# A decoder layer's first feed-forward product: from seven block products to plain tiles of 128 columns

## The chip, the cores and the metric

The kernel runs on one core of a Trainium2 chip. Its time is the device time of one execution in microseconds (us); the median of several executions is compared. TensorE multiplies (its stationary operand is loaded by separate weight loads), ScalarE and VectorE work element by element and read TensorE's results from PSUM, GpSimd (POOL in the profile) issues the DMAs that add, and SyncE (SP) issues the loads. Each engine has its own queue of instructions, which it works through in order.

## What is computed

One decoder layer on x of 512 positions by 1024 channels: two mixers, a merge, an output projection, a layer norm, and then a feed-forward block with a second layer norm. The change touches the feed-forward block only:

```python
    h = layer_norm(DEEPNORM_ALPHA * h + mix, ln1_g[l], ln1_b[l])
    f = jnp.square(jax.nn.relu(h @ w_ff1[l])) @ w_ff2[l]
    h = layer_norm(DEEPNORM_ALPHA * h + f, ln2_g[l], ln2_b[l])
```

w_ff1 is 1024 x 4096 and w_ff2 is 4096 x 1024, in float32. The kernel multiplies float32 numbers as pairs: each operand is split into a high part (a rounded copy) and a low part (the rest), and a product is three matmuls, high x high, high x low and low x high.

## The kernel before

**Stages.** Input projection, mixers and attention come first, then the output projection with the first layer norm (lines 740 to 852), then the feed-forward block in four quarters of 1024 hidden channels. In each quarter q the first product (FF1) makes the quarter's hidden values from h, and the second (FF2) adds their product with 1024 rows of w_ff2 to `hn`. Quarter 3's FF2 is not done in blocks but in plain steps (`b_step`, line 739), so that the layer norm can start early.

**Seven products.** A product of matrices that are cut into 2 x 2 blocks needs eight block products; both FF1 and FF2 use a scheme with seven, on sums of blocks. The seven are called p = 1 to 7. For FF1 the blocks of h (halves of channels by halves of positions) are copied and combined once, by `h_first` and `h_second`, into the pairs `X[p]`. The weight blocks come in column groups n of 512 columns, eight in all: `ff1_blocks` and `du_chunks` load each group into three tiles: U (two blocks, in the ring of buffers called raw), V (one block) and S (one block, twice). Sums are formed in place by DMAs that add, issued by POOL (`dma_add`): `s13` adds U's blocks to S; after the split for p = 1 S is added into U; after the split for p = 2 U is added into V. So each group has four adding DMAs, and the weights of p = 6, 7, 3 and 5 exist only when these have landed. FF2 does the same with blocks of w_ff2 (`ff2_blocks`), two halves h per quarter.

**Weight stream.** `Stream` holds a list of items in the order of use. `ws.get()` returns the next one's high and low parts and prepares two items ahead: `split` copies the float32 weights on ScalarE (line 150) and subtracts on VectorE (line 151), into one of three buffers `whi`, `wlo`. A tile is loaded when its ring has a free slot: raw, V and S have two each. In the time order of one engine everything queues: a load that waits for its slot holds back SP's later loads.

**FF1's products.** `ff1_product` (line 863) does 24 matmuls of 256 moving columns: two halves j of 128 weight columns, four channel tiles k, three matmuls each (lines 879, 881, 882). The moving operand is a block of h of 256 positions. The results of several p accumulate in one PSUM bank; ScalarE or VectorE takes them out, and `rest`, done one product later, applies relu and square and writes the blocks `Y[c]` of the hidden values that FF2 multiplies (`y_split`). A quarter has 14 such products. `ff2_product` (line 934) does per half h 12 matmuls of 512 columns (lines 947, 949, 950), and VectorE adds each p's two banks to `hn`.

**Order.** Tile's scheduler orders the instructions by their place in the program and its own model of times, so the last FF1 product of a quarter stands a few matmuls behind the first ones of FF2. Plain products with weights as the stationary operand use `dense_a` and `mm3` (lines 132 to 135): eight channel tiles of three matmuls with 512 moving columns:

```python
    def dense_a(ps, piece, mh, ml, c0=0, c1=S):
        hi, lo = piece
        for k in range(8):
            mm3(ps[:, c0:c1], hi[:, k], lo[:, k], mh[:, k, c0:c1], ml[:, k, c0:c1], k == 0, k == 7)
```

## Time and profile before

| | us |
|---|---|
| median of 3 runs (924.97 to 927.46) | 926.69 |
| the profiled execution | 929.51 |
| its span, from first to last instruction | 927.8 |
| TensorE busy | 884.8 |
| VectorE busy | 550.9 |
| ScalarE busy | 408.7 |
| GpSimd busy | 51.3 |

The profile is of one execution. Its span is the time from the first to the last instruction; the rest of the execution's time lies around it. Busy times of matmuls overlap, since TensorE starts one before the last has left it, so the pace of TensorE is read from the starts of its matmuls. A wait is put down to what came last of the things that an instruction waited for.

### The profile page before, as it was taken

The page shows a single profiled execution, that of the slowest core. Times are in us where ns is not written, and L with a number is a line of the kernel's source. Part 1 is how long each engine was busy: PE and PEld are TensorE (multiplying, and loading weights), DVE is VectorE, ACT ScalarE, POOL GpSimd, SP SyncE. Part 2 cuts the span into 40 slices and gives each one's busy share as a digit, 9 for nine tenths or more (in the row PEclk, how much of TensorE's full clock was granted, in tenths as well). Part 3 has the DMA queues.
Part 4 walks back from the last instruction along what each step waited for, and adds up shares of the span by engine and source line. Part 5 has one row for each costly group of instructions (what it writes and reads, how often), then busy time and mean ns, then how long its engine had stood idle before and what let it go on. Part 6 is the DMA issues. An engine that isn't in the chain of part 4 may idle for free. (4 is left out here: it accounts for less than half of the span.)

```text
span 927.8 us, 12312 instructions
## 1 busy us (share of the span) xinstructions
PE 884.8 (95%) x4792; PEld 759.1 (82%) x4792; DVE 550.9 (59%) x1039; ACT 408.7 (44%) x704; POOL 51.3 (6%) x68
## 2 busy tenths in 40 slices
PE   8999999999999999999999998998899989988996
PEld 6888898988887888888788888867887888778984
DVE  2322736442238766767556688784578467745667
ACT  2522313242226556555433146742665267426800
POOL 1000000000000000000000100111021102111000
PEclk9999999999999999999999998999899989998998
DMA  6458501232332111111383923969697969694601
GB/s 199 130 177 239 170 24 47 78 130 91 97 114 64 40 53 46 46 47 46 118 290 130 211 46 92 243 145 272 153 241 153 274 172 236 160 246 110 192 37 68
DMA packets 79865, 125.83 MB, mean 136 GB/s; under 512 B 3328, under 2 KB 55360, under 8 KB 79808
## 3 DMA queue, kind: packets, MB, share of 16 engines
q1 hardware_dynamic: 67232, 88.19, 29.0%
q0 software_dynamic: 8064, 29.36, 16.9%
q10 hardware_dynamic: 4512, 7.50, 2.6%
q8 instruction: 37, 0.61, 0.3%
q14 instruction: 20, 0.16, 0.0%
HBM read 93.59 MB, written 2.10 MB: 103 GB/s over the span
## 5 line engine op out<-in xcount | busy, mean ns | idle before, releaser
L151 DVE TENSOR_TENSOR wlo<-raw,whi 128x1024 fp32r<-128x1024 f32 (+3 forms) x125 | 145.2, 1165 | 184.9 <-ACT whi L150 184.2
L150 ACT ACTIVATE whi<-raw 128x1024 fp32r<-128x1024 f32 (+3 forms) x125 | 126.1, 1012 | 239.5 <-PE ps L134 115.4
L879 PE MATMUL ps<-x,whi 128*128 128x256 f32 x448 | 133.7, 299 | 18.3 <-ACT whi L150 10.1
L882 PE MATMUL ps<-x,wlo 128*128 128x256 f32 x448 | 132.7, 296 | 5.1 <-DVE wlo L151 5.1
L881 PE MATMUL ps<-x,whi 128*128 128x256 f32 x448 | 131.7, 294 | 1.6 <-DVE x L817 1.6
L133 PE MATMUL ps<-xh,whi 128*128 128x512 f32 x320 | 129.6, 405 | 0.0
L134 PE MATMUL ps<-xl,whi 128*128 128x512 f32 x320 | 125.7, 393 | 0.0
L135 PE MATMUL ps<-xh,wlo 128*128 128x512 f32 x320 | 125.7, 393 | 0.0
L879 PEld LDWEIGHTS ps<-x,whi 128*128 128x128 f32 x448 | 90.9, 203 | 22.5 <-ACT whi L150 11.4
L882 PEld LDWEIGHTS ps<-x,wlo 128*128 128x128 f32 x448 | 90.8, 203 | 6.6 <-DVE wlo L151 6.6
L881 PEld LDWEIGHTS ps<-x,whi 128*128 128x128 f32 x448 | 90.9, 203 | 2.2 <-DVE x L817 2.1
L135 PEld LDWEIGHTS ps<-xh,wlo 128*128 128x128 f32 x320 | 60.5, 189 | 13.2
L134 PEld LDWEIGHTS ps<-xl,whi 128*128 128x128 f32 x320 | 60.8, 190 | 9.5
L133 PEld LDWEIGHTS ps<-xh,whi 128*128 128x128 f32 x320 | 60.7, 190 | 9.5
L950 PE MATMUL ps<-wlo,y 128*128 128x512 f32 x144 | 56.9, 395 | 3.3 <-DVE wlo L151 3.3
L947 PE MATMUL ps<-whi,y 128*128 128x512 f32 x144 | 56.7, 394 | 1.4 <-ACT whi L150 1.4
L949 PE MATMUL ps<-whi,y 128*128 128x512 f32 x144 | 56.2, 390 | 0.0
L208 POOL DMA_DIRECT2D S<-raw x28 | 24.3, 890 | 568.9 <-DMA raw<-in_w_ff_dram 539.7
L628 ACT ACTIVATE PP<-PP,nm 128x512 f32<-128x512 f32 (+3 forms) x64 | 35.8, 559 | 35.6 <-DVE nm L622 35.3
L151 DVE TENSOR_TENSOR wlo<-S,whi 128x1024 fp32r<-128x1024 f32 x28 | 34.0, 1222 | 25.0 <-ACT whi L150 24.9
L151 DVE TENSOR_TENSOR wlo<-V,whi 128x1024 fp32r<-128x1024 f32 x28 | 34.2, 1223 | 21.4 <-ACT whi L150 20.5
L150 ACT ACTIVATE whi<-S 128x1024 fp32r<-128x1024 f32 x28 | 29.3, 1055 | 36.6 <-DMA S<-raw 15.8
(223 smaller groups left out, 1745.2 us busy)
## 6 DMA issues: line engine op xcount, KB each, us to landing
raw<-in_w_in_dram SPq DMA_DIRECT2D x17, 1024.0 KB, 5.2
S<-in_w_ff_dram SPq DMA_DIRECT2D x28, 512.0 KB, 6.0
raw<-in_w_ff_dram SPq DMA_DIRECT2D x28, 512.0 KB, 6.2
S<-raw POOLq DMA_DIRECT2D x28, 512.0 KB, 7.5
V<-in_w_ff_dram SPq DMA_DIRECT2D x14, 512.0 KB, 5.0
raw<-S POOLq DMA_DIRECT2D x14, 512.0 KB, 6.3
V<-raw POOLq DMA_DIRECT2D x14, 512.0 KB, 5.3
raw<-in_w_in_dram SPq DMA_DIRECT2D x8, 512.0 KB, 3.6
```

Source lines behind the costliest of these rows:

```text
L133: nc.tensor.matmul(ps, hi, mh, start=start, stop=False)
L134: nc.tensor.matmul(ps, hi, ml, start=False, stop=False)
L135: nc.tensor.matmul(ps, lo, mh, start=False, stop=stop)
L150: nc.scalar.activation(hi, r, AF.Copy)
L151: nc.vector.tensor_sub(lo, r, hi.bitcast(F32))
L628: nc.scalar.activation(t, t, AF.Exp, bias=nm[:, e, i:i + 1], scale=-1.0, accum_out=sm[:, e, i:i + 1])
L879: nc.tensor.matmul(o, hi[:, k, js], xh[:, k], start=opens and j == 0 and k == 0, stop=False, skip_group_check=True)
L881: nc.tensor.matmul(o, hi[:, k, js], xl[:, k], start=False, stop=False, skip_group_check=True)
L882: nc.tensor.matmul(o, lo[:, k, js], xh[:, k], start=False, stop=j == 1 and k == 3, skip_group_check=True)
L947: nc.tensor.matmul(ps, yh, hi[:, kk], start=opens and h == 0 and kk == 0, stop=False, skip_group_check=True)
L949: nc.tensor.matmul(ps, yl, hi[:, kk], start=False, stop=False, skip_group_check=True)
L950: nc.tensor.matmul(ps, yh, lo[:, kk], start=False, stop=h == 1 and kk == 1, skip_group_check=True)
```

## The change

FF1 gets plain tiles. The transposed h is kept whole, as `hTh` and `hTl` (8 channel tiles x 512 positions); `h_transpose` fills them with one copy and one subtraction per bank. A quarter has eight pieces of 128 hidden columns, each one `dense_a`: 24 matmuls of 512 columns (lines 133 to 135), accumulated in one bank. The weights come in loads of 1 MB, each for two pieces (`cols_a`), without sums of blocks: `ff1_blocks`, `ff1_product` and FF1's 32 adding DMAs are gone. From quarter 1 on the first two loads of a quarter go into the S ring, the other two into raw. In quarter 0 three pieces take their high and low parts in the slots of S and V (`early`), are multiplied with positions 0 to 255 first, and with 256 to 511 after the last two transposes. `ff1_evict` takes a piece out of PSUM with Relu and Square on ScalarE and, once per two pieces, writes the block sums `Y[c]` that FF2 wants: the same seven as before. FF2's code does not change. The four vectors of both layer norms are loaded together into `lnc`.

```diff
-    def add(shape, dmas, pieces):
-        c = ws.chunk("raw", shape, dmas)
+    def add(shape, dmas, pieces, ring="raw"):
+        c = ws.chunk(ring, shape, dmas)
...
-    def cols_a(w, c0, ncol, kt=8):
+    def cols_a(w, c0, ncol, kt=8, ring="raw", dsts=(None, None)):
...
-                pieces=[((lambda t, j=j: t[:, :, j * P:(j + 1) * P]), None) for j in range(2)]))
+                pieces=[((lambda t, j=j: t[:, :, j * P:(j + 1) * P]), dsts[j]) for j in range(2)], ring=ring))
...
-                ready=lambda: "lpool" in res)
+                ready=lambda: "rings" in res)
...
-    def ff1_blocks(n):
-        def blk(half, k):
-            c0 = 1024 * (n // 2) + 512 * half + 256 * (n % 2)
-            return w1v[:, 4 * k:4 * k + 4, c0:c0 + 256]
-        return du_chunks([4, 256], blk)
...
-    ffseq, FF2 = [], (1, 2, 6, 5, 7, 3, 4)
+    FF2 = (1, 2, 6, 5, 7, 3, 4)
+    def early():
+        res["early"] = res.get("early", 0) + 1
+        if res["early"] < 3:
+            t = res["lpool"].tile([P, 2, 8, P], F32R, tag="S", bufs=2, name=f"e{res['early']}")
+            return t[:, 0], t[:, 1]
+        hl = [res["lpool"].tile([P, 8, P], F32R, tag="V", bufs=2, name=f"e{res['early']}{i}")
+              for i in range(2)]
+        res["rings"] = True
+        return hl
...
-        du = [2 * q, 2 * q + 1]
...
-        ffseq.append([(2 * q + i, p) for i, p in order])
-        dus = {}
-        for n, p in ffseq[q]:
-            if n not in dus:
-                dus[n] = ff1_blocks(n)
-                du_item(dus[n], p, s13(dus[n]))
-            else:
-                du_item(dus[n], p)
+        for i, c in enumerate((0, 512, 256, 768)):
+            cols_a(w1, 1024 * q + c, 256, ring="S" if q and i < 2 else "raw",
+                   dsts=((early, early if i == 0 else None) if q == 0 and i < 2 else (None, None)))
...
-    def consts(g, b):
-        res["lnc"] = slab("lnc", [P, 2, D])
-        nc.sync.dma_start(res["lnc"][:, 0], bcast(g[0]))
...
+    lnc = slab("lnc", [P, 4, D])
+    for i, t in enumerate((ln1_g, ln1_b, ln2_g, ln2_b)):
+        nc.sync.dma_start(lnc[:, i], bcast(t[0]))
...
+    hTh = slab("hTh", [P, 8, S], F32R)
+    hTl = slab("hTl", [P, 8, S], F32R)
+    def h_transpose(t):
...
-    def x_split(p, src, cs, k4=slice(0, 4)):
-        h, l = X[p][0][:, k4, cs], X[p][1][:, k4, cs]
-        nc.scalar.activation(h, src, AF.Copy)
-        nc.vector.tensor_sub(l, src, h.bitcast(F32))
...
-    def h_first(t):
-        cs = slice(t * P, (t + 1) * P)
-        for p, raw, pt in zip((1, 2), (h11, h21), h_banks(t, "aa")):
-            x_split(p, pt, cs)
-            nc.scalar.activation(raw[:, :, cs], pt, AF.Copy)
...
-    def h_second(t, tags):
-        cs = slice((t - 2) * P, (t - 1) * P)
-        p0, p1 = h_banks(t, tags)
-        nc.scalar.activation(h22[:, :, cs], p1, AF.Copy)
-        t1, t3, t2, t4 = (small_t("T").rearrange("p (k i) -> p k i", k=4) for _ in range(4))
-        nc.vector.tensor_tensor(t1, h11[:, :, cs], p0, op=ALU.subtract)
-        nc.vector.scalar_tensor_tensor(t2, t1, -1.0, h22[:, :, cs], op0=ALU.mult, op1=ALU.subtract)
-        x_split(5, t1, cs)
-        x_split(6, t2, cs)
-        nc.vector.tensor_tensor(t3, h22[:, :, cs], p0, op=ALU.subtract)
-        x_split(3, h22[:, :, cs], cs)
-        nc.vector.scalar_tensor_tensor(t4, t2, -1.0, h21[:, :, cs], op0=ALU.mult, op1=ALU.subtract)
-        x_split(7, t3, cs)
-        x_split(4, t4, cs)
...
+            p3 = pt.rearrange("p (k i) -> p k i", k=4)
+            dh = hTh[:, 4 * q:4 * q + 4, t * P:(t + 1) * P]
+            dl = hTl[:, 4 * q:4 * q + 4, t * P:(t + 1) * P]
+            nc.scalar.activation(dh, p3, AF.Copy)
+            nc.vector.tensor_sub(dl, p3, dh.bitcast(F32))
...
         if t > 1:
-            h_first(t - 2)
...
+            h_transpose(t - 2)
...
+    y4 = lpool.tile([P, 2, D], F32R, tag="y4", bufs=1, name="y4")
+    RR = slab("RR", [P, 2, 2, 2, 512])
...
-    def ff1_product(n, p):
...
-        xh, xl = X[p]
-        for j in range(2):
-            js = slice(j * P, (j + 1) * P)
-            o = ps[:, j * 256:(j + 1) * 256]
-            for k in range(4):
-                nc.tensor.matmul(o, hi[:, k, js], xh[:, k], start=opens and j == 0 and k == 0, stop=False,
-                                 skip_group_check=True)
-                nc.tensor.matmul(o, hi[:, k, js], xl[:, k], start=False, stop=False, skip_group_check=True)
-                nc.tensor.matmul(o, lo[:, k, js], xh[:, k], start=False, stop=j == 1 and k == 3,
-                                 skip_group_check=True)
-        while later:
-            later.pop(0)()
-        if p in (1, 5, 6):
-            g[p] = small_t("b")
-            nc.scalar.activation(g[p], ps, AF.Copy)
...
+    def ff1_evict(q, i, ps, g):
+        if i % 4 == 0:
+            g["R"] = RR[:, i // 4]
+        R = g["R"]
+        r = lpool.tile([P, S], F32, tag="r", bufs=2, name=f"r{q}_{i}")
+        nc.scalar.activation(r, ps, AF.Relu)
+        nc.scalar.activation(R[:, i % 4 // 2, i % 2], r, AF.Square)
+        if i % 2 == 0:
             return
-        if p == 4:
-            t = g["t21"] = small_t("b")
-            nc.scalar.activation(t, ps, AF.Relu, scale=-1.0)
+        rows = slice(2 * (i // 4), 2 * (i // 4) + 2)
+        b11, b12, b21, b22 = (R[:, h, :, c:c + 256] for h in range(2) for c in (0, 256))
+        def y_split(c, t):
+            nc.scalar.activation(Y[c][0][:, rows], t, AF.Copy)
+            nc.vector.tensor_sub(Y[c][1][:, rows], t, Y[c][0][:, rows].bitcast(F32))
+        if i % 4 == 1:
+            y_split(1, b11)
+            if q == 3:
+                y_split(5, b12)
+            else:
+                nc.vector.tensor_sub(b11, b11, b12)
+                y_split(5, b11)
+        elif q == 3:
+            y_split(2, b21)
+            y_split(3, b22)
         else:
-            t = g[{2: 1, 3: 6, 7: 5}[p]]
-            nc.vector.tensor_add(t, t, ps)
-        rows = slice(2 * (n % 2), 2 * (n % 2) + 2)
-        def y_split(c, t):
-            t3 = t.rearrange("p (k i) -> p k i", k=2)
-            nc.scalar.activation(Y[c][0][:, rows], t3, AF.Copy)
-            nc.vector.tensor_sub(Y[c][1][:, rows], t3, Y[c][0][:, rows].bitcast(F32))
-        def rest():
-            if p != 4:
-                nc.scalar.activation(t, t, AF.Relu, scale=-1.0 if p == 7 else 1.0)
-            nc.scalar.activation(t, t, AF.Square)
-            t11, t12, t22 = g[1], g.get(6), g.get(5)
-            plain = n // 2 == 3
-            if p == 2:
-                y_split(1, t)
-            elif p == 3:
-                if plain:
-                    y_split(5, t)
-                else:
-                    nc.vector.tensor_sub(t11, t11, t12)
-                    y_split(5, t11)
-            elif p == 7:
-                y_split(3, t)
-                if not plain:
-                    nc.vector.scalar_tensor_tensor(t11, t11, -1.0, t22, op0=ALU.mult, op1=ALU.subtract)
-                    y_split(6, t11)
-                    nc.vector.tensor_sub(t12, t22, t12)
-                    y_split(7, t12)
-            else:
-                y_split(2, t)
-                if not plain:
-                    nc.vector.scalar_tensor_tensor(t, t11, -1.0, t, op0=ALU.mult, op1=ALU.subtract)
-                    y_split(4, t)
-        later.append(rest)
+            nc.vector.scalar_tensor_tensor(b11, b11, -1.0, b22, op0=ALU.mult, op1=ALU.subtract)
+            y_split(2, b21)
+            y_split(6, b11)
+            nc.vector.tensor_sub(b12, b22, b12)
+            y_split(7, b12)
+            nc.vector.scalar_tensor_tensor(b21, b11, -1.0, b21, op0=ALU.mult, op1=ALU.subtract)
+            y_split(3, b22)
+            y_split(4, b21)
...
     for q in range(4):
-        for i, (n, p) in enumerate(ffseq[q]):
-            if q == 0 and i in (1, 3):
-                h_second(2 + i // 2, ("bc", "dd")[i // 2])
-            ff1_product(n, p)
-        while later:
-            later.pop(0)()
+        g, i0 = {}, 0
+        if q == 0:
+            i0 = 3
+            pcs = [ws.get() for _ in range(3)]
+            bs = [bank("d"), bank("d"), bank("c")]
+            for i in range(3):
+                dense_a(bs[i], pcs[i], hTh, hTl, 0, 256)
+            for t in (2, 3):
+                h_transpose(t)
+            for i in range(3):
+                dense_a(bs[i], pcs[i], hTh, hTl, 256, 512)
+                ff1_evict(q, i, bs[i], g)
+        for i in range(i0, 8):
+            pc = ws.get()
+            ps = bank("b")
+            dense_a(ps, pc, hTh, hTl)
+            ff1_evict(q, i, ps, g)
...
-        consts(ln2_g, ln2_b)
```

The instructions' order shows what moves. **TensorE, quarter 0, at the transposes of the last tile of positions** (`ps` is a PSUM bank, `hn` the normalised h, `e` an early piece), before and after:

```order
L881 MATMUL ps_4566<-x_4202,whi_4470 128x256
L882 MATMUL ps_4566<-x_4202,wlo_4471 128x256
L809 MATMUL ps_4597<-ident,hn 128x128 x4
L809 MATMUL ps_4602<-ident,hn 128x128 x4
L879 MATMUL ps_4630<-x_4202,whi_4531 128x256
L881 MATMUL ps_4630<-x_4202,whi_4531 128x256
```

```order
L134 MATMUL ps_4475<-hTl,e_4449 128x256
L135 MATMUL ps_4475<-hTh,e_4450 128x256
L786 MATMUL ps_4562<-ident,hn 128x128 x4
L786 MATMUL ps_4569<-ident,hn 128x128 x4
L133 MATMUL ps_4473<-hTh,e_4178 128x256
L133 MATMUL ps_4474<-hTh,e_4181 128x256
L133 MATMUL ps_4475<-hTh,e_4449 128x256
L133 MATMUL ps_4666<-hTh,whi_4463 128x512
```

The eight transposes stand at the same place behind 72 matmuls of 256 columns; behind them come the second halves of the early pieces in place of the fourth block product.

**TensorE, from the end of quarter 0's FF2 to quarter 1's FF1**, before and after:

```order
L947 MATMUL ps_5023<-whi_5229,x_4466 128x512
L949 MATMUL ps_5023<-whi_5229,x_4466 128x512
L950 MATMUL ps_5023<-wlo_5230,x_4466 128x512
L879 MATMUL ps_5292<-x_4202,whi_5252 128x256
L881 MATMUL ps_5292<-x_4202,whi_5252 128x256
L882 MATMUL ps_5292<-x_4202,wlo_5253 128x256
```

```order
L867 MATMUL ps_4866<-whi_5069,y_4445 128x512
L869 MATMUL ps_4866<-whi_5069,y_4445 128x512
L870 MATMUL ps_4866<-wlo_5070,y_4445 128x512
L133 MATMUL ps_5130<-hTh,whi_5089 128x512
L134 MATMUL ps_5130<-hTl,whi_5089 128x512
L135 MATMUL ps_5130<-hTh,wlo_5090 128x512
```

FF1 has 512 moving columns instead of 256, and takes the whole of h instead of a block; no FF1 matmul stands inside an FF2 stage any more.

**SP's queue of loads, from quarter 0's FF2 to quarter 1's** (raw, V and S are the rings, with the number of the tile; x2 stands for two loads of 512 KB), before and after:

```order
L80 DMA V2_4691<-in_w_ff2_dram 128x2x512
L80 DMA S2_4723<-in_w_ff2_dram 128x2x512 x2
L80 DMA raw48_4789<-in_w_ff2_dram 128x2x512 x2
L80 DMA V3_4863<-in_w_ff2_dram 128x2x512
L80 DMA S3_4901<-in_w_ff2_dram 128x2x512 x2
L80 DMA raw49_4935<-in_w_ff2_dram 128x2x512 x2
L80 DMA S4_5148<-in_w_ff1_dram 128x4x256 x2
L80 DMA S5_5169<-in_w_ff1_dram 128x4x256 x2
L80 DMA V4_5188<-in_w_ff1_dram 128x4x256
L80 DMA V5_5208<-in_w_ff1_dram 128x4x256
L80 DMA raw50_5226<-in_w_ff1_dram 128x4x256 x2
```

```order
L80 DMA raw50_4707<-in_w_ff2_dram 128x2x512 x2
L80 DMA S0_4457<-in_w_ff2_dram 128x2x512 x2
L80 DMA S1_4460<-in_w_ff2_dram 128x2x512 x2
L80 DMA V0_4453<-in_w_ff2_dram 128x2x512
L80 DMA V1_4455<-in_w_ff2_dram 128x2x512
L80 DMA raw51_4781<-in_w_ff2_dram 128x2x512 x2
L80 DMA S2_4991<-in_w_ff1_dram 128x8x256
L80 DMA S3_5011<-in_w_ff1_dram 128x8x256
L80 DMA V2_5029<-in_w_ff2_dram 128x2x512
L80 DMA V3_5049<-in_w_ff2_dram 128x2x512
L80 DMA raw52_5067<-in_w_ff1_dram 128x8x256
L80 DMA raw53_5087<-in_w_ff1_dram 128x8x256
```

FF1's loads fall from five blocks of 512 KB per group of 512 columns to four, in units of 1 MB; two of each quarter's four go to S, ahead of V's blocks for the next FF2. POOL's queue keeps the adding DMAs of FF2 alone, 24 of 56.

## Rows read from the trace of the kernel before

**Rows 1.** The page's part on engines: busy time, share of the span, instructions.

```profile
PE 884.8 (95%) x4792; PEld 759.1 (82%) x4792; DVE 550.9 (59%) x1039; ACT 408.7 (44%) x704; POOL 51.3 (6%) x68
```

**Rows 2.** Windows: us, then busy us (count) of each engine, granted clock, DMA share, GB/s.

```profile
500.00:546.00 46.00, 46.00 (x209) 38.18 (x208) 32.51 (x68) 10.15 (x13) 4.46 (x5) 1.00 0.59 149
546.18:594.31 48.13, 43.65 (x338) 42.51 (x336) 44.62 (x68) 36.90 (x56) 4.25 (x5) 0.93 0.54 132
594.31:640.04 45.73, 42.80 (x195) 33.89 (x193) 31.99 (x39) 21.03 (x25) 6.81 (x8) 1.00 0.83 222
640.04:689.94 49.90, 41.82 (x314) 40.59 (x313) 27.75 (x33) 27.40 (x39) 6.97 (x9) 0.93 0.79 188
689.94:732.84 42.90, 42.02 (x195) 34.10 (x193) 32.05 (x39) 21.12 (x25) 7.04 (x9) 1.00 0.85 225
732.84:780.84 48.00, 41.99 (x314) 40.75 (x313) 27.71 (x33) 27.41 (x39) 6.57 (x9) 0.93 0.81 194
780.84:823.70 42.86, 41.97 (x195) 34.09 (x193) 29.63 (x37) 20.40 (x25) 5.77 (x7) 1.00 0.82 218
823.70:872.00 48.30, 41.84 (x314) 40.61 (x313) 25.36 (x27) 27.32 (x38) 5.94 (x7) 0.93 0.64 143
```

**Rows 3.** Timeline of TensorE: start, us, engine, line, operation, out<-in, shape.

```profile
502.44 0.39 PE L745 MATMUL ps<-whi,mh 128*128 128x512 f32 x1
...
533.04 0.39 PE L745 MATMUL ps<-oh,mh 128*128 128x512 f32 x1
...
566.68 0.41 PE L882 MATMUL ps<-x,wlo 128*128 128x256 f32 x1
...
570.73 0.41 PE L879 MATMUL ps<-x,whi 128*128 128x256 f32 x1
...
575.23 0.28 PE L879 MATMUL ps<-x,whi 128*128 128x256 f32 x1
...
594.19 0.28 PE L882 MATMUL ps<-x,wlo 128*128 128x256 f32 x1
```

**Rows 4.** TensorE's waits, 546 to 872: us in total, times, longest.

```profile
PE ps L879 <- ACT whi L150: 10.1, 6, 2.3
PE ps L879 <- ACT b L888: 5.3, 5, 2.0
PE ps L882 <- DVE wlo L151: 5.1, 7, 0.8
PE ps L950 <- DVE wlo L151: 3.3, 7, 0.5
PE ps L879 <- ACT x L816: 2.7, 1, 2.7
```

**Rows 5.** ScalarE's waits, 640 to 690 us.

```profile
ACT whi L150 <- DMA S<-raw: 8.8, 1, 8.8
ACT whi L150 <- DMA raw<-S: 6.6, 2, 5.8
```

**Rows 6.** DMA issues: queue, count, KB each, median us to landing.

```profile
raw<-in_w_ff_dram SPq DMA_DIRECT2D x28, 512.0 KB, 6.2
S<-raw POOLq DMA_DIRECT2D x28, 512.0 KB, 7.5
...
raw<-S POOLq DMA_DIRECT2D x14, 512.0 KB, 6.3
```

**Rows 7.** Groups by line: duration in ns, or busy us and mean ns.

```profile
L151 DVE TENSOR_TENSOR wlo<-S,whi 128x1024 fp32r<-128x1024 f32 x28 | 34.0, 1222 | 25.0 <-ACT whi L150 24.9
...
L150 ACT ACTIVATE whi<-S 128x1024 fp32r<-128x1024 f32 x28 | 29.3, 1055 | 36.6 <-DMA S<-raw 15.8
...
L816 ACT ACTIVATE x<-ps x4: 578/592/597, 537.8 to 547.9; 128x512 fp32r<-128x512 f32 x4
...
L817 DVE TENSOR_TENSOR x<-T,x x8: 680/684/693, 555.7 to 569.7; 128x512 fp32r<-128x512 f32 x8
L817 DVE TENSOR_TENSOR x<-ps,x x4: 636/654/673, 538.7 to 549.4; 128x512 fp32r<-128x512 f32 x4
```

More of the change, by code (lines that the diff above doesn't have):

```diff
@@ L253, in s13 @@
         return go
-    ffseq, FF2 = [], (1, 2, 6, 5, 7, 3, 4)
-    for q in range(4):
-        du = [2 * q, 2 * q + 1]
-        if q == 0:
-            order = [(0, 1), (0, 2), (1, 1), (1, 2), (0, 5), (0, 6), (0, 3), (0, 7), (1, 5), (0, 4), (1, 6),
-                     (1, 3), (1, 7), (1, 4)]
-        else:
-            order = [(0, 1), (0, 2), (0, 5), (0, 6), (0, 3), (0, 7), (1, 1), (0, 4), (1, 2), (1, 5), (1, 6),
-                     (1, 3), (1, 7), (1, 4)]
-        ffseq.append([(2 * q + i, p) for i, p in order])
-        dus = {}
-        for n, p in ffseq[q]:
-            if n not in dus:
-                dus[n] = ff1_blocks(n)
-                du_item(dus[n], p, s13(dus[n]))
-            else:
-                du_item(dus[n], p)
+    FF2 = (1, 2, 6, 5, 7, 3, 4)
[8 more added lines that the diff above has]
+        return hl
+    for q in range(4):
+        for i, c in enumerate((0, 512, 256, 768)):
+            cols_a(w1, 1024 * q + c, 256, ring="S" if q and i < 2 else "raw",
+                   dsts=((early, early if i == 0 else None) if q == 0 and i < 2 else (None, None)))
         if q < 3:
@@ L756, in norm_in, with norm_out @@
         nc.vector.bn_stats(st6[:, t, e], hn[:, t, cs])
-    def norm_out(t, eps, emit=None):
-        lnc = res["lnc"]
+    def norm_out(t, eps, gi, emit=None):
         n = 2 if emit is None else 4
@@ L766, in centre @@
                 cs = todo.pop(0)
-                nc.vector.scalar_tensor_tensor(hn[:, t, cs], hn[:, t, cs], mv[:, t, 0:1], lnc[:, 0, cs],
+                nc.vector.scalar_tensor_tensor(hn[:, t, cs], hn[:, t, cs], mv[:, t, 0:1], lnc[:, gi, cs],
                                                op0=ALU.subtract, op1=ALU.mult)
@@ L776, in norm_out @@
                 cs = slice(c * 512, (c + 1) * 512)
-                nc.vector.scalar_tensor_tensor(hn[:, t, cs], hn[:, t, cs], y, lnc[:, 1, cs],
+                nc.vector.scalar_tensor_tensor(hn[:, t, cs], hn[:, t, cs], y, lnc[:, gi + 1, cs],
                                                op0=ALU.mult, op1=ALU.add)
@@ L789, in layer_kernel @@
     last = [ws.get() for _ in range(6)]
-    def block(t, i):
-        return t[:, i].rearrange("p (k t) -> p k t", k=4)
-    X = {}
-    x12 = slab("x12", [P, 4, D], F32R)
-    X[1], X[2] = (block(x12, 0), block(x12, 1)), (block(x12, 2), block(x12, 3))
-    hraw = slab("hraw", [P, 4, D])
-    h11, h21, h22 = (block(hraw, i) for i in range(3))
-    def small_t(name):
-        state["id"] += 1
-        return lpool.tile([P, 512], F32, tag="bt", bufs=6, name=f"{name}{state['id']}")
-    def h_banks(t, tags):
-        pts = []
+    hTh = slab("hTh", [P, 8, S], F32R)
+    hTl = slab("hTl", [P, 8, S], F32R)
+    def h_transpose(t):
         for q in range(2):
-            pt = bank(tags[q])
+            pt = bank(("a", "b")[q])
             for k in range(4):
@@ L844, in layer_kernel, with block @@
             norm_in(t, e, ob, 2.0 * ALPHA)
-        norm_out(t, 4.0 * EPS)
+        norm_out(t, 4.0 * EPS, 0)
         if t > 1:
-            h_first(t - 2)
-    x56 = slab("x56", [P, 4, D], F32R)
-    x37 = slab("x37", [P, 4, D], F32R)
-    x4 = slab("x4", [P, 4, D], F32R)
-    for p, (t, i) in {5: (x56, 0), 6: (x56, 2), 3: (x37, 0), 7: (x37, 2), 4: (x4, 0)}.items():
-        X[p] = (block(t, i), block(t, i + 1))
+            h_transpose(t - 2)
+    def block(t, i):
+        return t[:, i].rearrange("p (k t) -> p k t", k=4)
     y12 = slab("y12", [P, 4, D], F32R)
@@ L986, in layer_kernel @@
                 norm_in(t, e, fb, 1.0)
-            norm_out(t, EPS, lambda cs: (nc.scalar if cs.start else nc.sync).dma_start(
+            norm_out(t, EPS, 2, lambda cs: (nc.scalar if cs.start else nc.sync).dma_start(
                 out[t * P:(t + 1) * P, cs], hn[:, t, cs]))
```

16 lines of the change are left out of this document (1 added, 15 removed).

## The prediction

> **What bounds the kernel now.** I read the profile from the outside in. First the busy shares: TensorE is busy 95% of the span [rows 1], but a matmul's busy time overlaps the next one's, so this only says that TensorE sets the end. Next the stretch that the change rewrites, 546.18 to 872.00 us, cut into its seven stages [rows 2]: four stages of the first feed-forward product (FF1, quarters 0 to 3) alternate with three of the second (FF2). The last of a quarter's 14 FF1 products lies a few matmuls inside the next window. Then the pace, from the starts of matmuls in the order of time [rows 3]: with 512 moving columns 135 starts take 30.60 us, 226.7 ns each; with 256 columns 158 starts take 18.96 us, 120.0 ns each. So half the columns cost 53%, not 50%. With 256 columns at the half clock 19 starts take 4.05 us, 213 ns each.
>
> Pace times count gives what a window should take; the rest is lost. FF1 of quarters 1 to 3 has 312 matmuls of 256 columns in its window, 37.44 us; the windows are 49.90, 48.00 and 48.30 us, so 12.5, 10.6 and 10.9 us are lost. FF1 of quarter 0 takes 48.13: 37.44 are matmuls, 3.0 transposes, 7.7 lost. An FF2 window holds 168 matmuls of 512 columns (38.09) and 24 of 256 (2.88), 40.97 us, and takes 45.73, 42.90 and 42.86: 4.8, 1.9 and 1.9 lost. About 50 us of the stretch are lost, two thirds of it in the last three FF1 stages. Who is waited for [rows 4]: mostly ScalarE's split of the next weight block (10.1 us before line 879) and its eviction of a product from PSUM (5.3). The granted clock is 0.93 in every FF1 window and 1.00 in every FF2 window [rows 2]: each FF1 stage also pays for its pauses with matmuls at the 1.2 GHz level.
>
> Why the split is late is on ScalarE's own list for 640 to 690 us [rows 5]: it waited 8.8 us for a DMA into S from raw and 6.6 for one into raw from S, the accumulating DMAs that form the block sums of FF1. Each moves 512 KB and lands 6.3 to 7.5 us after its issue, and a load that it needs lands after 6.2 [rows 6]. When a quarter's FF2 ends, the buffers for the next FF1 are only just being filled and added up.
>
> **FF1's matmuls: dearer.** Before, 8 column groups x 7 products x 24 matmuls of 256 columns: 1344 x 0.120 = 161.3 us. After, 32 pieces x 24 matmuls of 512 columns, the first three pieces in two halves of 256: 696 x 0.2267 + 144 x 0.120 = 175.1 us. That alone is +13.8 us on the engine that sets the end.
>
> The Trainium skill, "TensorE: Matmul & The Clock Gate", section "Back-to-back issue gap", gives an isolated gap of N/2.4 + 2.5 ns: 109 ns for 256 columns and 216 for 512. The trace disagrees at both, by 11 ns: 120 and 227 [rows 3]. By the page the change would cost 19.2 us here instead of 13.8, as the fixed part would weigh less in the narrow matmuls; the forecast would come out 5.4 us later. I go by the rows, which show both shapes in this kernel.
>
> **FF1's waits in quarters 1 to 3: mostly gone.** A plain piece needs one load and one split, with no accumulating DMA ahead of it. The order of the instructions shows that the first two loads of 1 MB for the next FF1 go into the S slots, directly behind the FF2 loads, and that POOL's queue keeps 24 adding DMAs of 56. The S slots are free when FF2's product 7 has been split. Counted in FF2 steps of 12 matmuls (2.72 us) with two steps of lead, that is 18.6 us after FF2 begins for the first slot and 21.3 for the second. FF1 begins at 38.1 and splits its first piece two steps earlier, at 32.7; even with two 6.2 us loads after one another the first lands at 25 and the second at 31, and the second is first split at 38. ScalarE then has per piece a split (1.06) and, averaged, about 3.75 operations of some 0.6 (Relu, Square and 7 splits of y per four pieces): 3.3 us in 5.44. VectorE has 1.22 and 11 operations of some 0.7 per four pieces: 3.1 us [rows 7]. Both stay under the piece's 24 x 0.2267 = 5.44, so nothing there is next in line, and with no pause the clock stays up as it does in the FF2 windows. Each stage: 192 x 0.2267 = 43.5 us. Before, with the 14th product: 52.8, 50.9, 51.2. **Gain 154.8 - 130.6 = 24.3 us.** Bounds: the FF2 windows, which have weights ready and 512 columns, lose 1.9 to 4.8 in 168 matmuls, so nothing to 4 us per stage; I take nothing, because those losses stand behind accumulating DMAs, which these pieces do not have.
>
> **FF1 of quarter 0.** TensorE's row order is the same up to the last eight transposes: 72 matmuls of 256 columns stand ahead of them in both. I keep that part, 546.18 to 559.05, 12.9 us. After the transposes the second halves need the copy of the first bank (0.59) and the subtraction (0.65) [rows 7]: a new wait of about 1.3 us (zero to the 2.7 us that the first x block of quarter 0 waits now [rows 4]). Then 72 x 0.120 = 8.6 and five pieces, 27.2. Together 50.0 us against 48.13 + 2.88 = 51.0. **Gain 1.0 us.** The first four pieces are split while the output projection still runs, some three splits (3.7 us of VectorE) more than before in a stretch where VectorE is busy 32.5 of 46 us [rows 2]: hidden in its 13 idle microseconds; if not, the normalisation and the transposes behind it come up to 2 us later. The two extra loads of the second layer norm's constants stand in SP's queue ahead of an output weight that SP cannot issue for another 10 us anyway: nothing.
>
> **FF2.** Its code is the same, its surroundings are not. Its V and S blocks are loaded earlier (after three early pieces V's ring belongs to FF2 alone, and S is free once two pieces are done), and FF1's adding DMAs no longer compete. Without the FF1 product the windows take 42.85, 40.02 and 39.98 us, against 38.1 by pace. Quarter 0's 4.8 us lost should come down to what the others lose, and theirs partly go too. I take 39.3 for each, between 38.1 (nothing lost) and the 122.85 of now. **Gain 122.85 - 117.9 = 4.9 us.**
>
> **Sum.** 24.3 + 1.0 + 4.9 = 30.2 us. The profiled execution took 929.51 us around a span of 927.8: 899.3 after. It lies 2.8 us above the median of the runs, 926.69; against that, 896.5, and I say **897 us**. Outside the stretch the order on TensorE is the same. The low end: FF2 by pace (3.6 less) and no wait in quarter 0 (1.3): 892. The upper end of this case: FF2 as it is now (5.0 more) and some 3 us for the waits that I set at zero: 905.
>
> **The rivals.** *FF2 by pace alone.* If all accumulations come early enough, FF2 loses nothing: 892. For it: a third of FF1's DMA work goes. Against: some of FF2's waits [rows 4] are for VectorE, which keeps its queue of y subtractions just there. Chance 0.12.
>
> *The wait moves into the load of plain pieces.* SP issues in order; if the S slots come free only when product 7's split has waited for its own accumulation, each FF1 starts late, pauses, and pays for the half clock again. A third of what the three stages lose now, 11.3 us, would stay: 908. Against it: about 7 us of spare time in the count above. Chance 0.11.
>
> *FF2's second half is starved.* The raw slot of its second block is freed only by the split of FF1's last piece, 14 us before FF2 starts. From there the chain is a load (6.2), an add into S (7.5), an add back into raw (6.3) and the split (2.3): 22.3 us, and product 6's second half needs it 14 + 13.6 = 27.6 us on. The margin is 5 us. At 10 us of wait in each of the three FF2 stages the gain is used up (896.5 + 30 = 926.5); from 11 us on, a chain of some 39 us, the kernel is slower, and at 14 us each it takes 938.5. The DMA share of 0.83 to 0.85 in FF2 windows [rows 2] speaks for long adds, the third of the adds' traffic that is left speaks against. Chance 0.04 for slower, 0.03 for a draw near 927.
>
> **Chances.** The forecast 0.70 (892 to 905), FF2 by pace 0.12 (890 to 893), the moved wait 0.11 (905 to 914), FF2 starved 0.07. The range from 891 to 907 holds all of the first, most of the second and a little of the third, about 0.82. A difference of 0.3%, 2.8 us, is about what a measurement of this kernel can tell from none: faster 0.93, the same 0.03, slower 0.04.
>
> **What the profile after would show.** Right, if matmuls of FF1 start 227 ns apart, the FF1 windows of quarters 1 to 3 take 43.5 to 45 us at clock 1.00, ScalarE's list of waits there names TensorE and no accumulating DMA, and the FF2 stages take 38 to 40 us each. Wrong, if TensorE waits at the first or third piece of an FF1 for a load (the moved wait), if FF2's product 6 waits for a DMA into raw from S (starved), or if the 512-column matmuls run slower than 227 ns beside the DMAs.

## The result, and the profile after

| | before | after |
|---|---|---|
| median of runs taken side by side (4 each), us | 925.83 (924.24 to 927.46) | 893.88 (893.62 to 894.17) |
| the profiled execution | 929.51 | 893.99 |
| its span | 927.8 | 892.3 |
| TensorE busy | 884.8 | 878.0 |
| VectorE busy | 550.9 | 500.4 |
| ScalarE busy | 408.7 | 367.8 |
| GpSimd busy | 51.3 | 24.3 |

The ratio is 0.9655, with a 95% interval of 0.9636 to 0.9674: 32 us less. The page of after, its part on engines (busy us, share of the span, instructions) and its chain of work that ended last, by engine:

```profile
PE 878.0 (98%) x4288; PEld 734.0 (82%) x4288; DVE 500.4 (56%) x977; ACT 367.8 (41%) x644; POOL 24.3 (3%) x36
...
PE 97%; DVE 1%; DMA 1%; ACT 0%; issue 0%; SPq 0%; DVEq 0%; ACTq 0%
```

TensorE's busy time fell by 6.8 us only [rows 1], the span by 35.5: TensorE stood for 43.0 us of the span before and for 14.3 after. The busy time fell although FF1's matmuls are 13.8 us dearer by pace, so some 20 us of slowed matmuls went as well (an estimate, 6.8 + 13.8). The windows of after, one per stage, with the columns of [rows 2] (FF1 of quarter 0, then FF2 and FF1 in turn; all of FF1 now lies in its own window):

```profile
545.70:594.30 48.60, 47.61 (x290) 42.05 (x288) 24.96 (x42) 21.94 (x36) 4.46 (x5) 1.00 0.58 160
594.30:632.54 38.24, 38.24 (x170) 31.52 (x168) 29.75 (x35) 18.64 (x22) 2.59 (x3) 1.00 0.66 182
632.54:676.06 43.52, 43.52 (x194) 36.04 (x192) 19.64 (x24) 21.61 (x32) 4.30 (x5) 1.00 0.60 156
676.06:714.33 38.27, 38.27 (x169) 31.54 (x168) 29.75 (x35) 18.64 (x22) 2.56 (x3) 1.00 0.66 181
714.33:757.85 43.52, 43.52 (x193) 36.05 (x192) 19.64 (x24) 21.61 (x32) 4.30 (x5) 1.00 0.60 155
757.85:796.09 38.24, 38.24 (x169) 31.53 (x168) 29.74 (x35) 18.64 (x22) 2.58 (x3) 1.00 0.59 155
796.09:839.61 43.52, 43.52 (x193) 36.05 (x192) 14.46 (x16) 19.81 (x29) 0.00 (x0) 1.00 0.19 62
```

192 matmuls at the 226.7 ns of [rows 3] are 43.53 us: the FF1 stages run at pace to a hundredth of a microsecond, the FF2 stages (168 matmuls, 38.09) to 0.2 us, and the granted clock is 1.00 in every window, where the FF1 windows of before had 0.93. The list of what TensorE waited for between 540 and 875 us (in total, times, longest) answers to [rows 4], and has two entries:

```profile
PE ps L134 <- DVE hTl L792: 0.7, 1, 0.7
PE ps L133 <- ACT hTh L791: 0.3, 1, 0.3
```

ScalarE's list for 632 to 676 us answers to [rows 5]. No adding DMA is in it; its splits now wait for TensorE to give a buffer back, which is the right way round:

```profile
ACT whi L150 <- PE ps L134: 14.5, 6, 4.4
ACT y L829 <- DVE RR L837: 3.0, 2, 1.5
```

### The profile page after: what moved, and what is told of

It reads as the page before. It is cut to its first block, busy times and chain, and to the rows that moved or that the text cites. A ratio compares the mean times of both kernels' runs of the same rounds, so it can differ in the third digit from the quotient of the medians.

```text
span 892.3 us, 10986 instructions
## 1 busy us (share of the span) xinstructions
PE 878.0 (98%) x4288; PEld 734.0 (82%) x4288; DVE 500.4 (56%) x977; ACT 367.8 (41%) x644; POOL 24.3 (3%) x36
## 4 chain that ended last, share of the span: by engine, by line
PE 97%; DVE 1%; DMA 1%; ACT 0%; issue 0%; SPq 0%; DVEq 0%; ACTq 0%
PE ps L133 19%; PE ps L135 19%; PE ps L134 19%; PE ps L867 4%; PE ps L870 4%; PE ps L869 4%; PE ps L737 3%; PE ps L735 3%; PE ps L736 3%; PE ps L662 2%; PE ps L414 2%; PE ps L412 2%; PE ps L457 2%; PE ps L413 2%; PE ps L677 1%; PE ps L679 1%
## 5 line engine op out<-in xcount | busy, mean ns | idle before, releaser
L133 PE MATMUL ps<-hTh,whi 128*128 128x512 f32 x232 | 90.3, 389 | 0.0
L134 PE MATMUL ps<-hTl,whi 128*128 128x512 f32 x232 | 90.3, 389 | 0.0
L135 PE MATMUL ps<-hTh,wlo 128*128 128x512 f32 x232 | 90.3, 389 | 0.0
L867 PE MATMUL ps<-whi,y 128*128 128x512 f32 x168 | 65.5, 390 | 0.0
L870 PE MATMUL ps<-wlo,y 128*128 128x512 f32 x168 | 65.5, 390 | 0.0
L869 PE MATMUL ps<-whi,y 128*128 128x512 f32 x168 | 65.5, 390 | 0.0
L135 PEld LDWEIGHTS ps<-hTh,wlo 128*128 128x128 f32 x232 | 43.6, 188 | 9.1
L134 PEld LDWEIGHTS ps<-hTl,whi 128*128 128x128 f32 x232 | 43.5, 188 | 9.0
L133 PEld LDWEIGHTS ps<-hTh,whi 128*128 128x128 f32 x232 | 43.6, 188 | 8.9
L621 ACT ACTIVATE PP<-PP,nm 128x512 f32<-128x512 f32 (+3 forms) x64 | 35.8, 560 | 35.5 <-DVE nm L615 35.2
L830 DVE TENSOR_TENSOR y<-RR,y 128x512 fp32r<-128x512 f32 x50 | 33.1, 689 | 16.0 <-ACT y L829 16.0
L870 PEld LDWEIGHTS ps<-wlo,y 128*128 128x128 f32 x168 | 31.5, 188 | 6.8
```

What stands on the lines that cost most here:

```text
L133: nc.tensor.matmul(ps, hi, mh, start=start, stop=False)
L134: nc.tensor.matmul(ps, hi, ml, start=False, stop=False)
L135: nc.tensor.matmul(ps, lo, mh, start=False, stop=stop)
L621: nc.scalar.activation(t, t, AF.Exp, bias=nm[:, e, i:i + 1], scale=-1.0, accum_out=sm[:, e, i:i + 1])
L830: nc.vector.tensor_sub(Y[c][1][:, rows], t, Y[c][0][:, rows].bitcast(F32))
L867: nc.tensor.matmul(ps, yh, hi[:, kk], start=opens and h == 0 and kk == 0, stop=False, skip_group_check=True)
```

## The experiments

The theory: what FF1 of quarters 1 to 3 loses stands behind its adding DMAs (load, add, add, split), and the clock behind the pauses. The first rival: ScalarE and VectorE are too loaded in FF1 for the splits to come in time. A second question was whether FF1's matmuls got dearer by what the rows said, a third why FF2 gained too. In the medians below, before stands at 926.3 to 927.0, measured beside each kernel.

**Before without FF1's adding DMAs, without part of the evictions, and without both.** In the first kernel FF1's blocks are multiplied as loaded; in the second relu, square and the block sums of the hidden values are left out of the evictions, while the adding DMAs stay.

```diff
 # e1 and e3: FF1's calls of du_item, without s13 too
-            if p == 1:
+            if p == 1 and adds:
                 dma_add(u(1), s(0))
-            if p == 2:
+            if p == 2 and adds:
                 dma_add(v(), u(1))
 # e2 and e3: in rest()
-            if p != 4:
-                nc.scalar.activation(t, t, AF.Relu, scale=-1.0 if p == 7 else 1.0)
-            nc.scalar.activation(t, t, AF.Square)
```

> The kernel before, with the 32 adding DMAs of FF1 left out (the weight sums are not formed; every load, split, matmul and eviction stays). Theory A, the chain of adding DMAs makes FF1 wait: the FF1 windows of quarters 1 to 3 fall from 49.9, 48.0 and 48.3 us to 38 to 40 (pace 37.4) at clock 0.98 or more, and the kernel comes to some 890 us, below the changed kernel's 893.9, since the seven products are 13.8 us cheaper by pace. Theory B, ScalarE and VectorE are the limit of the narrow products (per seven products of 2.88 us, 20.2 us, ScalarE has 7 splits and 18 operations of some 0.62, 18.6 us or 92%; VectorE 18.1 or 90%): only the waits at the start of each quarter go, some 5 us with their half clock per quarter, and the kernel stays at 905 to 912 with FF1 windows of 42 to 45.

> The kernel before, with relu, square and the four block sums of the hidden values left out of FF1's evictions (the copies and the splits of y stay): ScalarE's load per seven products falls from 18.6 to 14.2 us of 20.2, VectorE's from 18.1 to 15.4; the adding DMAs stay. Theory A: FF1 windows of quarters 1 to 3 stay within 2 us of 49.9, 48.0, 48.3; the kernel takes 918 to 926. Theory B: they fall to 40 to 44, the kernel to 900 to 910.

> The kernel before with both left out, FF1's adding DMAs and relu, square and block sums. Both theories: FF1 windows near the pace, 38 to 39 us, kernel 880 to 888. If A alone is right it equals the run without adding DMAs to within 3 us; if B alone, it equals the run with light evictions to within 5; if each alone keeps over 10 us of loss, both limits bind in turn.

Measured: 892.38 us without the adds (ratio 0.9648, 0.9613 to 0.9683), 931.1 with light evictions (1.0051, 1.0021 to 1.0081), 897.46 with both (0.9698, 0.9658 to 0.9738). Windows of the kernel without FF1's adds, FF2 of quarter 0, FF1 of quarter 1, FF2 of quarter 1, columns as above:

```profile
594.07:639.53 45.46, 43.56 (x195) 35.29 (x193) 32.24 (x39) 21.25 (x26) 4.94 (x6) 0.96 0.82 219
639.53:676.96 37.43, 37.43 (x313) 37.43 (x312) 27.95 (x33) 27.77 (x39) 1.89 (x3) 1.00 0.53 155
676.96:719.56 42.60, 41.72 (x194) 34.09 (x193) 32.21 (x39) 21.14 (x26) 4.94 (x6) 1.00 0.81 210
```

The FF1 window holds 312 matmuls of 256 columns in 37.43 us, 120.0 ns each; it took 49.90 with the adds [rows 2]. ScalarE and VectorE have the same 28 us of work in it as before, and nothing waits for them. The theory stands: the adds, and the clock that the pauses cost, are all that these stages lose. The load of the two engines is not the cause, for a lighter load alone made nothing faster. That kernel came out a little slower: FF1 of quarter 1 took 51.96 us there. In FF2 of quarter 0 ScalarE stood 9.4 us behind one add into raw, where it had stood 3.8, but the split behind that add came no later in the stage (19.4 us after its begin, 19.2 before); ScalarE only reached it sooner. Why the kernel is slower was not followed. The kernel with both edits missed the 880 to 888 that both theories gave: its FF1 windows are 37.43 us, as without the adds alone, but FF2 of quarters 0 and 1 took 47.31 and 43.27 us instead of 45.46 and 42.60. That is outside FF1, and its cause stays open.

**After with FF1's matmuls in halves.** Each piece of the changed kernel is multiplied with positions 0 to 255 and then with 256 to 511.

```diff
-            dense_a(ps, pc, hTh, hTl)
+            dense_a(ps, pc, hTh, hTl, 0, 256), dense_a(ps, pc, hTh, hTl, 256, 512)
```

> The changed kernel with every piece of FF1 multiplied in two halves of 256 columns (twice the matmuls and weight loads, the same loads, splits and evictions): 1392 more narrow in place of 696 wide matmuls. If FF1 is bound by TensorE's pace alone: 1392 x 0.120 - 696 x 0.2267 = +9.3 us, 903. If the narrow matmuls had a loss of their own in the kernel before (more weight loads, the clock): 905 or more, with a clock below 0.99 in the FF1 windows.

Measured: 903.06 us (0.9745, 0.9722 to 0.9768), 9.2 more than the changed kernel; each FF1 stage of quarters 1 to 3 takes 46.07 us for 384 matmuls, 120.0 ns each, without a wait. So half the columns cost 53% here also with no stall near, and the price of FF1's matmuls in the prediction is right. The gap that the Trainium skill, "TensorE: Matmul & The Clock Gate", section "Back-to-back issue gap", gives for an isolated matmul would have two halves 2.5 ns dearer than one whole, by my estimate 0.5 us per stage; the run, a stream of matmuls with a weight load each, shows 13.3 ns and 2.55 us.

**After without FF2's adding DMAs.** FF2's blocks are multiplied as loaded.

```diff
-                    du_item(dus[h], p, s13(dus[h]) if p == 1 else None)
+                    du_item(dus[h], p, adds=False)
```

> The changed kernel with FF2's 24 adding DMAs left out (FF2's weight sums are not formed). If FF2's chain of adds is wholly hidden, as its windows of 38.24 us at the pace say: no difference, 893 to 894.5. If adds slow TensorE's or the other engines' access to memory beside the waits: 1 to 3 us less.

Measured: 893.36 us (0.9641, 0.9614 to 0.9668), every stage as in the changed kernel (38.24 and 43.52). The 24 adds that are left cost nothing.

**Before without FF2's adds, and without any.** The same edit in the kernel before, alone and together with FF1's.

> The kernel before without FF2's 24 adding DMAs (FF2's blocks are multiplied as loaded), FF1's 32 stay. Theory (FF2 loses to its own adds): the FF2 stages lose under 0.5 us each instead of 4.8, 1.9 and 1.9, about 918. If the FF2 adds also hold back the slots of the next FF1, its first products come earlier too: down to 905. Rival (the hand-over on VectorE and ScalarE): FF2 as before, 924 to 928.

> The kernel before without any adding DMA, in FF1 or FF2 (blocks are multiplied as loaded, sums of weight blocks left out). Without FF1's alone it took 892.4, and the FF2 stages still lost 4.4, 1.5 and 1.2 us. Theory (what FF2 still loses stands behind its own adds): each FF2 stage loses under 0.5 us, the kernel takes 885 to 887. Rival (VectorE's and ScalarE's work at the hand-over from FF1, where the last product's evictions and splits of y are queued ahead of the next splits of weights): the losses stay, 891 to 893.

Measured: 918.72 us without FF2's (0.9928, 0.99 to 0.9957), 886.84 without any (0.9574, 0.9536 to 0.9612). Without any adds TensorE's list of waits from 590 to 840 us is empty, and the windows of FF2 of quarter 0, FF1 and FF2 of quarter 1 are:

```profile
593.98:635.35 41.37, 41.37 (x194) 34.26 (x193) 32.40 (x39) 21.27 (x26) 0.00 (x0) 1.00 0.45 145
635.35:672.78 37.43, 37.43 (x313) 37.43 (x312) 27.55 (x33) 27.87 (x39) 0.00 (x0) 1.00 0.38 128
672.78:714.12 41.34, 41.28 (x195) 34.36 (x193) 32.62 (x39) 21.27 (x26) 0.00 (x0) 1.00 0.43 139
```

(Each FF2 window holds FF1's last product too, 2.88 us.) VectorE and ScalarE do the same work in FF2 as before, and still nothing is lost: what FF2 lost stood behind its own adds too (without these alone its stages take 41.87, 41.18 and 41.35 us, against 40.97 by pace), although the waits' names in [rows 4] say VectorE (wlo before line 950). FF1's adds cost before 33.9 us, FF2's 7.7, both together 39.6.

**After with adding DMAs put back.** Each FF1 load of quarters 1 to 3 that is named gets two chained adds of 512 KB within its tile, ahead of its first split: all four loads of a quarter, the last two, or the first two.

```diff
+    def block_sums(t):
+        dma_add(t[:, 0:4], t[:, 4:8])
+        dma_add(t[:, 4:8], t[:, 0:4])
```

> The changed kernel with two chained adding DMAs of 512 KB on each 1 MB load of FF1 in quarters 1 to 3 (half of the tile added to the other half and back; the sums are wrong weights), 24 in all, ahead of the load's first split. If an adding chain costs its landing time beyond the stream's lead of two pieces (2 x 5.8 + 2.3 = 13.9 us against 10.9): some 3 us per load, 12 loads, 930 us. If early loads hide it: only the first load of a quarter is late (lands 25 us into FF2, sums at 37, wanted at 36), 894 to 900.

> The changed kernel with two chained adding DMAs on the last two of the four FF1 loads of quarters 1 to 3, those in the raw ring (12 in all; the sums are wrong, so the output is too). With them on all four loads it took 913.6. Theory (what counts is the lead of a chain before its use, and only the first load of a quarter is short of it): the FF1 windows stay at 43.5 and the kernel at 893 to 896. Rival (FF2's second block, whose raw slot comes free only with the split of the last piece, has little margin): the last pieces or FF2's product 6 wait, FF2 windows of 40 to 44 us, 900 to 908.

> The same two chained adding DMAs on the first two of the four FF1 loads of quarters 1 to 3 alone, those in the S ring (12 in all; the sums are wrong, so the output is too). Theory (the lead decides): the whole loss of the run with all four, three waits at the first pieces of 4 to 5 us and some 3 us each behind them: 910 to 916. Rival (the number of adding DMAs and their traffic decide): half of that loss, 902 to 905.

Measured: 913.61 us with adds on all loads (0.9856, 0.9819 to 0.9892), 892.78 on the last two (0.9638, 0.9617 to 0.9659), 912.34 on the first two (0.9844, 0.9824 to 0.9865). Twelve adds cost nothing or 18 us by where they stand. In the run with the late adds FF1 of quarter 1 has DMA engines busy for 0.83 of the time and stays at pace, with no wait of TensorE from 592 us on:

```profile
592.12:630.37 38.25, 38.25 (x170) 31.52 (x169) 29.74 (x35) 18.63 (x22) 3.42 (x4) 1.00 0.70 189
630.37:673.88 43.51, 43.51 (x193) 36.03 (x192) 19.62 (x24) 21.45 (x32) 6.84 (x8) 1.00 0.83 196
```

With the early adds TensorE's list from 592 to 880 us has one entry, the first piece of each of three quarters; its windows around the first of them follow (the last 4.6 us of FF2 with the wait, the 5.4 us behind it, the rest of FF1), and then ScalarE's list for 605 to 640 us:

```profile
PE ps L133 <- ACT whi L150: 10.7, 3, 4.2
...
630.00:634.62 4.62, 0.46 (x3) 0.03 (x1) 0.02 (x1) 1.11 (x2) 0.00 (x0) 0.87 1.06 257
634.62:640.00 5.38, 5.34 (x12) 3.75 (x13) 4.76 (x5) 1.96 (x2) 0.00 (x0) 0.50 0.81 227
640.00:681.11 41.11, 41.11 (x182) 34.00 (x181) 17.62 (x21) 20.54 (x31) 4.29 (x5) 1.00 0.58 149
...
ACT whi L150 <- DMA S<-S: 12.2, 2, 10.5
```

After a wait of 4.2 us the granted clock is 0.50, the 1.2 GHz level, for the 5.4 us that follow, and this FF1 window takes 46.49 instead of 43.52: each wait is paid once as a wait and again, by 2 to 3 us, as slow matmuls. 10.7 us of waits became 18. The run with adds on all loads met the number of neither expectation; the two later runs say why: only the head of a stage lacks lead, and there the lack is large. The adds on these first loads took 8.5 us from issue to landing (median), where the expectation had counted 5.8, and 6.5 on the last two. (The ring changes with the place: S for the first loads, raw for the last.)

**Before with more lead.** FF1 of quarters 1 to 3 takes quarter 0's order, in which four products instead of two stand ahead of the first added block.

```diff
-        if q == 0:
+        if q < 4:
             order = [(0, 1), (0, 2), (1, 1), (1, 2), (0, 5), ...]
```

> The kernel before, with quarter 0's order of FF1 products in all quarters: both column groups' products 1 and 2 first, so four products (11.5 us) instead of two (5.8 us) stand ahead of the first weight block that is formed by adding DMAs. Theory (the chain load, add, add, split is late by a fixed time when a quarter begins): 5.8 us more lead takes away most of the waits of FF1 in quarters 1 to 3, its windows come to 40 to 44 us instead of 48 to 50, and the kernel takes 903 to 912. If the lead were worth all of it, the windows would be 37.5 to 38 and the kernel would pass the changed one: 892 or less. Rival: the second group's loads now stand ahead in SP's queue and need slots that are not free, so the first group's adds come no sooner: windows as before, 924 to 930.

Measured: 927.98 us (1.002, 0.9996 to 1.0043): no difference. Timeline of ScalarE in FF1 of quarter 1 (start, us, engine, line, operation, out<-in; in brackets the idle time before it and what ended it):

```profile
650.25 1.06 ACT L150 ACTIVATE whi<-raw 128x1024 fp32r<-128x1024 f32 x1 [4.48 <-DMA raw<-S]
651.21 0.58 ACT L888 ACTIVATE b<-ps 128x512 f32<-128x512 f32 x1
656.25 1.06 ACT L150 ACTIVATE whi<-V 128x1024 fp32r<-128x1024 f32 x1 [4.46 <-DMA V<-raw]
...
660.01 0.58 ACT L888 ACTIVATE b<-ps 128x512 f32<-128x512 f32 x1
```

TensorE's list for this stage (636 to 683 us) has:

```profile
PE ps L879 <- ACT b L888: 5.1, 1, 5.1
PE ps L882 <- DVE wlo L151: 0.8, 1, 0.8
```

The short waits at the start of the stage [rows 4] are gone; a single long one takes their place, for the eviction at 660.01 (line 888). That eviction did not need any add: it stood in ScalarE's queue behind the split that did. The FF1 windows became 45.81, 46.27 and 50.92 us: 4.1 and 1.7 us shorter, and 2.6 longer in quarter 3, where the same wait took 9.1. FF2 of quarters 1 and 2 lost 1.6 to 1.8 us more, and nothing was left. The time is the rival's, but not its reason, for the windows did change; the theory's 40 to 44 us were not reached. Why FF2 lost more was not followed.

**Before with the sums formed by GpSimd itself.** This looked like a way to keep both FF1's cheaper matmuls and short chains.

```diff
-        nc.gpsimd.dma_start(dst..., src..., accum_op=ALU.add)
+        nc.gpsimd.tensor_tensor(dst, dst, src, op=ALU.add)
```

> The kernel before, whole, with its 56 block sums of weights formed by GpSimd's own elementwise add of 128x1024 numbers in place of an adding DMA. GpSimd's nearest operation in the trace of before, a select over 128x1024, took 1.09 us; an adding DMA landed 6.3 to 7.5 us after its issue. Theory (what FF1's seven products lose is the length of the chain load, add, add, split): if the add takes 1 to 2.5 us, each link is 4 to 6 us shorter, most of the waits go, and the kernel comes to 887 to 900; without any adding DMA it took 886.8, which is the floor. Below 893 it passes the changed kernel. Rival (the adds are late for another reason, their place in GpSimd's queue behind loads and splits, or GpSimd's add slows the other engines): 910 to 930.

Measured: 965.21 us (1.0429, 1.0405 to 1.0453), slower by 39. GpSimd's adds by line, then four of VectorE's groups for 600 to 750 us, of this kernel (busy us, mean ns of one, idle before it):

```profile
L208 POOL TENSOR_TENSOR S<-S,raw 128x1024 f32<-128x1024 f32 x28 | 83.5, 3005 | 559.0 <-DMA raw<-in_w_ff_dram 530.3 <-DVE y L900 28.7
...
L208 POOL TENSOR_TENSOR V<-V,raw 128x1024 f32<-128x1024 f32 x14 | 36.7, 2618 | 54.8 <-DVE wlo L151 32.7 <-issue 19.2 <-DVE rs L332 3.0
...
L151 DVE TENSOR_TENSOR wlo<-V,whi 128x1024 fp32r<-128x1024 f32 x12 | 21.3, 1772 | 9.6 <-ACT whi L150 9.6
L955 DVE SCALAR_TENSOR_TENSOR hn<-hn,ps 128x512 f32<-128x512 f32 x26 | 17.2, 680 | 0.1
L900 DVE TENSOR_TENSOR y<-b,y 128x512 fp32r<-128x512 f32 x17 | 16.4, 985 | 0.7 <-ACT y L899 0.6
L921 DVE TENSOR_TENSOR b<-b,b 128x512 f32<-128x512 f32 x3 | 8.6, 2876 | 0.0
```

and the same groups of the kernel before:

```profile
L151 DVE TENSOR_TENSOR wlo<-V,whi 128x1024 fp32r<-128x1024 f32 x13 | 15.9, 1223 | 9.6 <-ACT whi L150 8.8 <-PE ps L950 0.8
L956 DVE SCALAR_TENSOR_TENSOR hn<-hn,ps 128x512 f32<-128x512 f32 x28 | 18.5, 682 | 0.2
L901 DVE TENSOR_TENSOR y<-b,y 128x512 fp32r<-128x512 f32 x16 | 10.6, 686 | 0.9 <-ACT y L900 0.9
L922 DVE TENSOR_TENSOR b<-b,b 128x512 f32<-128x512 f32 x3 | 2.1, 685 | 0.0
```

An add took 2.6 to 3.0 us, shorter than the DMA. But the three groups of VectorE's operations on two operands from SBUF that are shown became 1.4 to 4.2 times as long, while the one that reads PSUM (hn<-hn,ps) stayed at 0.68. These means mix operations beside an add with others, and what counts is which starts first. Of this kernel's 28 wlo<-V,whi the 22 that met no add took 1.21 to 1.23 us, the six that started while one ran 3.39 to 3.42. Of the 18 b<-b,b beside an add the 11 that started while it ran took 2.83 to 2.90 us, the seven that started up to 0.25 us ahead of it 0.68 or 0.69. With b<-b,ps it was 0.67 to 0.69 either way. Two wlo<-V,whi in a row, and the add that the second one met:

```profile
616.80 1.23 DVE L151 TENSOR_TENSOR wlo<-V,whi 128x1024 fp32r<-128x1024 f32 x1 [0.36 <-ACT whi L150]
618.54 3.42 DVE L151 TENSOR_TENSOR wlo<-V,whi 128x1024 fp32r<-128x1024 f32 x1
...
618.10 2.78 POOL L208 TENSOR_TENSOR V<-V,raw 128x1024 f32<-128x1024 f32 x1 [4.02 <-DVE wlo L151]
```

The half of the rival that said GpSimd slows the other engines came true; what share of the 39 us it explains was not measured. The expectation's 1 to 2.5 us for an add was a little low.

## Why the prediction was right, and where it was off

**The sign and the size.** Faster by 3.4%: 893.9 us lie inside the range of 891 to 907 and 3 us under the 897.

**FF1's matmuls dearer, 13.8 us: right.** 226.7 ns per matmul in the windows of after; the halves run gives the price of the other shape free of stalls.

**FF1's waits in quarters 1 to 3, 24.3 us: right, and for the reason given.** Three windows of 43.52 make 130.6, as in the sum. The first S load is issued at 612.94, 18.6 us after FF2 begins, as counted. That the clock comes back by itself when the pauses go is seen too.

**FF1 of quarter 0, 1.0 us: too small, by 1.4.** The window is 48.60 instead of 50.0. The new wait of 1.3 us behind the last transposes is 0.25 us in the timeline of TensorE:

```profile
557.14 1.03 PE L786 MATMUL ps<-ident,hn 128*128 128x128 f32 x8
558.42 0.62 PE L133 MATMUL ps<-hTh,e 128*128 128x256 f32 x3 [0.25 <-ACT hTh L791]
558.88 0.40 PE L133 MATMUL ps<-hTh,whi 128*128 128x512 f32 x1
559.15 0.39 PE L134 MATMUL ps<-hTl,e 128*128 128x256 f32 x1
```

I had set that term at the copy plus the subtraction. The three matmuls at 558.42 and the one of 512 columns behind them do not need the subtraction, and the copy was nearly done when the eighth transpose was: the term is the tail of the copy, next to its lower bound of zero. The first part, up to the transposes' end, is 0.4 us shorter than the 12.9 that I kept.

What this stage lost before, 7.7 us, did not stand behind the adds: without any of them the stage takes 48.20 us (48.13 before). Its window and TensorE's waits in it, in the kernel without any adds:

```profile
545.78:593.98 48.20, 43.73 (x338) 42.57 (x337) 44.60 (x68) 36.86 (x56) 0.00 (x0) 0.93 0.28 95
...
PE ps L879 <- ACT x L816: 2.7, 1, 2.7
PE ps L881 <- DVE x L817: 1.6, 2, 0.8
```

TensorE waited for the combined blocks of h (`x`), and the clock fell to 0.93 here too. Plain tiles need no such blocks. By pace the stage now takes 3.0 + 144 x 0.120 + 120 x 0.2267 = 47.5 us, so 1.1 are lost. The change thus removed two kinds of sums, of weights in quarters 1 to 3 and of h in quarter 0.

**FF2, 4.9 us: too small, by 3.2.** The stages take 38.24, 38.27 and 38.24, not 39.3. This is the step that failed: I kept 1.2 us per stage because some of FF2's waits named VectorE, with its queue of y subtractions. The run of before without any adds has that queue and no such wait. The name of the engine that came last was not the cause; the add ahead of the split that VectorE follows was. The rival "FF2 by pace alone" had the mechanism right, and its 892 is only 2 us off.

FF2 keeps its own 24 adds, and they cost nothing now because they come sooner. The last add of quarter 0's FF2 in the kernel before, in that kernel without FF1's adds, and in the changed one:

```profile
613.91 0.85 POOL L208 DMA_DIRECT2D V<-raw  x1 [3.34 <-issue]
...
612.80 0.86 POOL L208 DMA_DIRECT2D V<-raw  x1 [3.34 <-issue]
...
603.16 0.86 POOL L208 DMA_DIRECT2D V<-raw  x1 [3.63 <-DVE wlo L151]
```

That is 19.6, 18.7 and 8.9 us into the stage. So of the two reasons that the prediction gave, FF1's adds being gone was worth only 0.3 to 0.6 us per stage (45.46, 42.60 and 42.30 instead of 45.73, 42.90 and 42.86). The rest goes with the earlier loads of V and S, which no run moved by themselves.

**The base.** By its own base, 899.3 against the profiled 893.99, the sum was 5.3 us too high, of which the two terms above are 4.6. By the medians it is off by 3, since the 2.8 us that the profiled execution of before lay above its median did not stay: after's lies 0.1 above its own. Those 2.8 us may have been losses of the kind that the change removed, which vary from one execution to the next: before's runs spread over 3.2 us, after's over 0.6. That is read from the spread alone, and not shown; the kernel of before without any adding DMA still spreads over 4.0 us (885.65 to 889.68), which speaks against it.

**The rivals that did not come.** The moved wait came only when two chained adds were put on the first loads of a quarter: then TensorE waits at the first piece, as described, and the kernel takes 912, near the 908 given. FF2's second half is not starved: the FF2 windows stay at pace, with a DMA share of 0.59 to 0.66 where before had 0.82 to 0.85.

**What stays open.** Plain pieces at the head of each quarter and seven products in its later part would have lead where it is needed. A column group takes 168 x 0.1200 = 20.2 us by seven products and 96 x 0.2267 = 21.8 by plain pieces: 1.6 us each, some 5 us if one of the two groups in quarters 1 to 3 goes back. It was not tried. It would need the combined blocks of h again (four more pairs, 32 KB per partition) beside the changed kernel's buffers, and quarter 0's waits for them could come back.
